# Decoder layer with 32 experts on one core: first norm applied in place, two more ring slots and one working slot lent to the weight ring's first turn, the loop for overfull experts moved from behind pair 3 to behind pair 11

## The chip, the cores and the metric

The kernel runs on one core of a Trainium2 chip. The metric is the device time of one execution in microseconds, as the median of three runs. All matrix work is in float32 or in a split float32 form, and all weights come from HBM once: 471 MB of them are read in one execution.

## The reference, cut to what matters

One attention sublayer and one mixture-of-experts sublayer, each followed by a layer norm. 256 tokens, 2048 features, 16 heads, 4 groups of 8 experts, 512 hidden features in an expert.

```
x = layer_norm(ALPHA * x + moba_attention(x, w_qkv, w_o), mix_ln_g, mix_ln_b)
# hierarchical_moe: best group of 4, then the best two of its 8 experts
comb = onehot_g[:, :, None] * e_gate[:, None, :]
for g in range(4):
    h = silu(einsum('td,edf->tef', xt, w_gate[g])) * einsum('td,edf->tef', xt, w_up[g])
    y = y + einsum('tef,efd->td', h * comb[:, g, :, None], w_down[g])
x = layer_norm(ALPHA * x + y, ffn_ln_g, ffn_ln_b)
```

So every token goes through 2 of 32 experts, 512 choices in all, and which tokens an expert gets is known only on the chip.

## The kernel before, in words

SBUF is cut into 24 slots of 128 x 2048 float32 (8 KB in each partition, 1 MB in all), named by tags (`slot`, L62). The attention half uses them for x, for its two split halves, for the heads' outputs, and seven of them as a ring for attention weights. The change is in the second half.

**The experts in pairs.** Sixteen pairs of experts run one after another (the loop `for p in range(NP)`). Each expert takes at most 64 tokens in this pass (CAP), so a pair fills 128 rows. One pair does, in TensorE's order: side 0's gate and up products in four steps j (`gate_up`, L511 to 516, tile gu), side 1's in four steps, the gather of the next pair's tokens in eight steps c2 (`gather`, L476, tiles pg and xg), the transpose of the hidden rows (hp, ht), and the down product in four steps k (L684, tile y). The rows of y are put back to their tokens by two more products for each half of the tokens (`add_rows`, `scatter`, tile cb) and added to the running sum; that is `rest(n)`, and it runs between the j steps of the next pair's side 0.

**The gather.** It is a matrix product: the normalised x is the stationary operand (the weights, 128 tokens by 128 features), and the 0/1 matrix o (tokens by slots, from `onehots`) is the moving one. Expert weights lie in HBM so that partition a of chunk (n, c) holds feature 512n + 4a + c. So the gather needs, as one weight block, the 128 features 4 apart. In the kernel before, ScalarE writes the normalised x to two other slots (xn, L404), and reads xs by steps of 4 so that each block lies in one run.

**The weight ring.** Each pair needs 24 pieces of 1 MB: 16 of gate and up, 8 of down; the last pair's down weights are 6 pieces of 1 MB and 4 of half of one. SP issues all their transfers in this order on one queue. `ring2` is 18 slots used in turn; `used(2)` behind each step of gate/up and each k of down gives two slots back, and `advance` issues the next pieces into them. An issue waits for the last reader of its slot, and for the transfer eight before it, since eight DMA semaphores are used in turn.

**The order.** TensorE and SP run in the written order from L647 on (`manual_schedule`); before it, the first pair's eight gathers and the count of overfull experts are written ahead of the pair loop and placed by the scheduler.

**The loop for overfull experts.** An expert with more than 64 tokens needs further passes (`further_passes`, L587). Their number is read on every engine; it is 0 for this input. The loop stands behind pair 3 (LOOP_AFTER = 2). Before it, all four rests of pair 3 run at once, four ring slots are kept free (LOOP_SLOTS), and all engines meet in a barrier.

**The rest.** `residual(j)` (L559) forms ALPHA * norm(x) + bias in xs, with rows of the norm's gain and bias made by TensorE (`rows_of`, L548); it runs in pair 1's side 0. The rows of the second norm (tiles r, copied to wv) are made in the last pair's side 1. "Pair 1" to "pair 16" count from one here; p in the code counts from zero.

Of the kernel before, what the change touches and what calls it, by code (L numbers as in the profile page):

```python
# [9 lines left out]
F32R = mybir.dt.float32r  # L10
# [17 lines left out]
WARM1 = (108, 16)  # L28
LOOP_AFTER = 2
LOOP_SLOTS = 4  # L30
# [8 lines left out]

S_XN, S_XG, S_YS = S_OH, 12, 13  # L40
S_EARLY, S_LATE = S_XH + S_XL + S_QK + (S_V,), S_OL + (14, S_TMP)
# [12 lines left out]
def hybrid_kernel(ctx: ExitStack, tc: tile.TileContext, x, w_qkv, w_o, ln1_g, ln1_b, w_grp, b_grp,  # L54
# [307 lines left out]
    done = (48 + sum(NCH * w // D for _, w in blocks)) % len(S_RING)  # L362
    ring2 = Rot(S_EARLY + S_RING[done:] + S_RING[:done] + S_LATE)
    n_ring = len(ring2.items)
# [8 lines left out]
    pieces += [(("v", 2, 0), None), (("v", 3, 0), None)]  # L373
# [3 lines left out]
    held, n_used = {}, 0  # L377

    def load(srcs, name, i=None):
        shape = [P, D] if srcs is None else list(srcs[0].shape) if len(srcs) == 1 else [P, len(srcs), *srcs[0].shape[1:]]  # L380
        t = slot(ring2() if i is None else i, shape, name)
# [4 lines left out]
    def advance(room=None):  # L386

        while len(held) < len(pieces) and len(held) - n_used < (room or n_ring):
            key, srcs = pieces[len(held)]
            held[key] = load(srcs, "w{}{}_{}".format(*key))  # L390

    def used(n, room=None):
        nonlocal n_used
        n_used += n
        advance(room)

# [159 lines left out]

    arstd = t2("arstd")

    def residual(n):  # L559

        cs = slice(n * 512, (n + 1) * 512)
        g_ = rows_of(0, n, yb[(2 * n) % 4], f"g1_{n}")
        b_ = rows_of(1, n, yb[(2 * n + 1) % 4], f"b1_{n}")
        for tt in range(NT):
            i = slice(tt, tt + 1)
            nc.vector.scalar_tensor_tensor(xs[tt][:, cs], xs[tt][:, cs], negmu[:, i], g_, op0=ALU.add, op1=ALU.mult)
            nc.vector.scalar_tensor_tensor(xs[tt][:, cs], xs[tt][:, cs], arstd[:, i], b_, op0=ALU.mult, op1=ALU.add)

    def gates():
# [13 lines left out]
        nc.vector.tensor_mul(gate, bc(ohg, GRP, EPG), le0.unsqueeze(2).to_broadcast([P, NT, GRP, EPG]))  # L583
        nc.vector.tensor_scalar_mul(arstd, rstd, ALPHA)
        return gate.rearrange("p t g e -> p t (g e)")

    def further_passes(free):  # L587

        ring = Rot(free[1:])
        n_pass = nc.values_load(passes_i[0:1, 0:1], min_val=0, max_val=8,  # L590
                                skip_runtime_bounds_check_because="512 choices in passes of 64 leave at most 7")
        with tc.For_i(0, n_pass, 1, iteration_sync="staggered"):  # L592
# [20 lines left out]
            one = bass.ds(er, 1)  # L613
            spare = slot(free[0], [P, 1024], "spare")
            xgx = spare.rearrange("p (n e s) -> p n e s", n=NCH, e=1)
# [21 lines left out]

    ys_all = slot(S_YS, [P, 2, 2, 512], "ys_all", F32R)
# [4 lines left out]
    gatef = gates()  # L643
    for tt in range(NT):
        nc.tensor.matmul(rps[:, 2, :], ones_b, selv[:, tt, :], start=tt == 0, stop=tt == 1)
    count_passes()
    order.enter_context(tc.manual_schedule(engines={mybir.EngineType.PE, mybir.EngineType.SP}))  # L647

    rest = None
    for p in range(NP):  # L650
        gu = [bank(gub(), [P, 512], f"gu{p}_{i}") for i in range(2)]
        hs = sm.tile([P, 512], F32, name=f"hs{p}", tag="ptv")
        for side in range(2):
            e = 2 * p + side
            for j in range(4):
                gate_up(gu[side], side, lambda c: xg[:, c, side], j, held["g", e, j], held["u", e, j])
                used(2, n_ring - (LOOP_SLOTS if p == LOOP_AFTER else 0))
# [18 lines left out]
        else:  # L676
            ht = transpose_hidden(hs, p)
        if p == NP - 1:
            break
        y = [bank(yb[n], [P, 512], f"y{p}_{n}") for n in range(4)]  # L680
        for k in range(4):
            for n in range(4):
                for side in range(2):
                    nc.tensor.matmul(y[n][sides[side]], ht[:, k, sides[side]], held["d", 2 * p + side, k][:, n * 512:(n + 1) * 512],  # L684
                                     start=k == 0, stop=k == 3, skip_group_check=True)
            used(2, n_ring - (LOOP_SLOTS if p == LOOP_AFTER else 0))

# [7 lines left out]
        if p == LOOP_AFTER:  # L695
            for n in range(4):
                rest(n)
            rest = None
            further_passes([ring2() for _ in range(LOOP_SLOTS)])
            ring2.n -= LOOP_SLOTS  # L700
            advance()
# [8 lines left out]
    def last_down(n):  # L710
# [7 lines left out]
        ys = slot((*S_XN, S_XG, S_YS)[n % 4], [P, 2, 512], f"ys{p}_{n}", F32R)  # L718
        split_rows(y, ys, width)
        lys.append(ys)  # L720

    def last_add(n):
        col, width = blocks[n]
        cs, ys = slice(col, col + width), lys[n]
        for tt in range(NT):
            cb = bank(last_cob(), [P, 512], f"cb{p}_{col}_{tt}")
            scatter(cb, ot, ys, tt, width)
            if n < ACT_STATS:
                st = stats2[:, tt, n]
                nc.vector.scalar_tensor_tensor(xs[tt][:, cs], cb[:, 0:width], 1.0, xs[tt][:, cs], op0=ALU.mult, op1=ALU.add,  # L730
                                               accum_out=sums[:, tt, n:n + 1])
                nc.vector.tensor_scalar_mul(st[:, 1:2], sums[:, tt, n:n + 1], 1.0 / width)
                nc.scalar.activation(cb[:, 0:width], xs[tt][:, cs], AF.Square, scale=-1.0, bias=st[:, 1:2], accum_out=st[:, 2:3])  # L733
            else:
                i = 2 * n - ACT_STATS
                nc.vector.tensor_add(xs[tt][:, cs], xs[tt][:, cs], cb[:, 0:width])
                nc.vector.bn_stats(stats2[:, tt, i:i + 2].rearrange("p a s -> p (a s)"), xs[tt][:, cs])

# [88 lines left out]
```

## Time and profile before

| | |
|---|---|
| median of 3 runs | 1403.14 us (1402.96 to 1406.17) |
| the profiled execution | 1405.03 us |
| its span, first to last instruction | 1403.3 us |
| TensorE busy in matmuls | 1348.7 us (96%) |
| VectorE, ScalarE, GpSimd busy | 450.5, 333.8, 16.3 us |
| granted TensorE clock, mean | 0.987 |
| DMA engines | 339 GB/s over the span, 421 GB/s in the second half |

The profile was taken in one execution, so its spans are compared with its own 1405.03 us; what lies outside the span is 1.7 us. A matmul's end is modelled, so 96% busy does not mean that TensorE has no slack: the chain of waits tells where it stood for a transfer. A float32 product is two passes, so the counts of rows in the trace are twice those of the code. DMA at 421 GB/s is the most that is seen over a long stretch.

### The profile page before, as it was taken

The page shows a single profiled execution, that of the slowest core. Times are in us where ns is not written, and L with a number is a line of the kernel's source. Part 1 is how long each engine was busy: PE and PEld are TensorE (multiplying, and loading weights), DVE is VectorE, ACT ScalarE, POOL GpSimd, SP SyncE. Part 2 cuts the span into 40 slices and gives each one's busy share as a digit, 9 for nine tenths or more (in the row PEclk, how much of TensorE's full clock was granted, in tenths as well). Part 3 has the DMA queues.
Part 4 walks back from the last instruction along what each step waited for, and adds up shares of the span by engine and source line. Part 5 has one row for each costly group of instructions (what it writes and reads, how often), then busy time and mean ns, then how long its engine had stood idle before and what let it go on. Part 6 is the DMA issues. An engine that isn't in the chain of part 4 may idle for free.

```text
span 1403.3 us, 17929 instructions
## 1 busy us (share of the span) xinstructions
PE 1348.7 (96%) x7537; PEld 807.7 (58%) x7537; DVE 450.5 (32%) x798; ACT 333.8 (24%) x567; POOL 16.3 (1%) x39
## 2 busy tenths in 40 slices
PE   9999999999999999979999999999999999998994
PEld 8999898988896534424344343443435434344442
DVE  5454645455454222221212212222122221212206
ACT  4454435345333101101011110110101101011123
POOL 0000100000000000000000000000000000000002
PEclk9999999999999999999999999999999999999997
DMA  9745455576555999989999999999999999999992
GB/s 340 239 151 182 148 171 190 180 262 239 176 200 218 365 421 421 421 357 421 421 421 421 420 421 421 421 421 421 421 421 421 421 421 421 421 421 421 420 382 71
DMA packets 103016, 475.52 MB, mean 339 GB/s; under 512 B 12756, under 2 KB 18964, under 8 KB 54804
## 3 DMA queue, kind: packets, MB, share of 16 engines
q1 hardware_dynamic: 102932, 474.33, 85.1%
q8 instruction: 61, 1.00, 0.3%
q14 instruction: 23, 0.19, 0.0%
HBM read 472.20 MB, written 2.10 MB: 338 GB/s over the span
## 4 chain that ended last, share of the span: by engine, by line
PE 41%; DMA 12%; DVE 2%; ACT 0%; issue 0%; DVEq 0%; SPq 0%; ACTq 0%
PE gu L516 19%; PE y L684 11%; DMA wu<-in_moe_w_up_dram 10%; PE pg L483 6%; PE cb L538 2%; DMA wd<-in_moe_w_down_dram 2%; PE cb L539 1%; PE y L716 1%; DVE xg L490 1%; PE r L553 1%; DVE xs L770 0%; DVE xs L760 0%; ACT cb L733 0%; DVE xs L756 0%; PE m L503 0%
## 5 line engine op out<-in xcount | busy, mean ns | idle before, releaser
L516 PE MATMUL gu<-wu,xg 128*64 128x512 f32 x1024 | 463.0, 599 | 16.1 <-DMA wu<-in_moe_w_up_dram 16.1
L516 PE MATMUL gu<-wg,xg 128*64 128x512 f32 x1024 | 462.1, 599 | 6.0 <-PEq L592 6.0
L516 PEld LDWEIGHTS gu<-wg,xg 128*64 128x64 f32 x1024 | 133.9, 137 | 205.6 <-issue 199.0
L684 PE MATMUL y<-wd,ht 128*64 128x512 f32 x960 | 209.3, 594 | 0.0
L516 PEld LDWEIGHTS gu<-wu,xg 128*64 128x64 f32 x1024 | 133.6, 137 | 90.1 <-issue 52.9
L160 PE MATMUL pj<-xh,ws 128*128 128x256 f32 x512 | 147.7, 288 | 0.8 <-ACT ws L150 0.8
L162 PE MATMUL pj<-xh,ws 128*128 128x256 f32 x512 | 147.3, 288 | 0.2 <-DVE ws L151 0.2
L161 PE MATMUL pj<-xl,ws 128*128 128x256 f32 x512 | 147.4, 288 | 0.0
L151 DVE TENSOR_TENSOR ws<-w,ws 128x1024 fp32r<-128x1024 f32 x88 | 107.8, 1225 | 122.2 <-ACT ws L150 122.2
L684 PEld LDWEIGHTS y<-wd,ht 128*64 128x64 f32 x960 | 67.6, 137 | 130.3 <-issue 127.9
L546 DVE TENSOR_TENSOR xs<-xs,cb 128x512 f32<-128x512 f32 x120 | 77.1, 683 | 192.6 <-PE cb L539 192.6
L483 PE MATMUL pg<-o,xn 128*128 128x128 f32 x1024 | 131.5, 281 | 4.3 <-DVE xg L490 2.4
L483 PEld LDWEIGHTS pg<-o,xn 128*128 128x128 f32 x1024 | 119.2, 191 | 28.4 <-issue 14.6
L150 ACT CAST ws<-w 128x1024 fp32r<-128x1024 f32 x88 | 92.4, 1050 | 135.1 <-PE pj L162 132.4
L532 ACT CAST ys_all<-y 128x512 fp32r<-128x512 f32 x60 | 35.1, 585 | 312.7 <-PE y L684 175.2
L521 DVE SCALAR_TENSOR_TENSOR hs<-hs,gs,gu 64x512 f32<-64x512 f32 x32 | 23.9, 747 | 239.2 <-ACT hs L520 237.9
L160 PEld LDWEIGHTS pj<-xh,ws 128*128 128x128 f32 x512 | 99.5, 194 | 1.2 <-ACT ws L150 1.0
L162 PEld LDWEIGHTS pj<-xh,ws 128*128 128x128 f32 x512 | 99.5, 194 | 0.8 <-DVE ws L151 0.6
L161 PEld LDWEIGHTS pj<-xl,ws 128*128 128x128 f32 x512 | 99.5, 194 | 0.1
L533 DVE TENSOR_TENSOR ys_all<-y,ys_all 128x512 fp32r<-128x512 f32 x60 | 41.2, 687 | 170.6 <-ACT ys_all L532 168.5
L490 DVE TENSOR_SCALAR xg<-pg,gbp 128x128 f32<-128x128 f32 x128 | 46.6, 405 | 91.9 <-PE pg L483 91.9
L520 ACT ACTIVATE hs<-gu 64x512 f32<-64x512 f32 x32 | 18.9, 591 | 218.1 <-PE gu L516 217.7
(196 smaller groups left out, 1251.9 us busy)
## 6 DMA issues: line engine op xcount, KB each, us to landing
wg<-in_moe_w_gate_dram SPq DMA_DIRECT2D x128, 1024.0 KB, 19.8
wu<-in_moe_w_up_dram SPq DMA_DIRECT2D x128, 1024.0 KB, 19.8
wd<-in_moe_w_down_dram SPq DMA_DIRECT2D x120, 1024.0 KB, 19.8
w<-in_attn_w_qkv_dram SPq DMA_DIRECT2D x44, 1024.0 KB, 5.1
wow<-in_attn_w_o_dram SPq DMA_DIRECT2D x16, 1024.0 KB, 5.2
wl<-in_moe_w_down_dram SPq DMA_DIRECT2D x6, 1024.0 KB, 17.2
wfirst<-in_attn_w_qkv_dram SPq DMA_DIRECT2D x3, 1024.0 KB, 11.3
xs<-in_x_dram SPq DMA_DIRECT2D x8, 256.0 KB, 8.6
```

What stands on the lines that cost most here:

```text
L150: nc.scalar.copy(t[:, 0, c], src[:, c])
L151: nc.vector.tensor_sub(t[:, 1, c], src[:, c], t[:, 0, c].bitcast(F32))
L160: nc.tensor.matmul(dst, ah, bh, start=start, stop=False, **kw)
L161: nc.tensor.matmul(dst, ah, bl, start=False, stop=False, **kw)
L162: nc.tensor.matmul(dst, al, bh, start=False, stop=stop, **kw)
L483: nc.tensor.matmul(pg[:, cc], xn[tt][:, n, c, :], o2[:, tt].rearrange("p e s -> p (e s)"), start=tt == 0, stop=tt == 1)
L490: nc.vector.tensor_scalar(to, pg[:, cc], g_, b_, op0=ALU.mult, op1=ALU.add)
L516: nc.tensor.matmul(gu[to], xg(4 * j + c), w[:, c, :], start=st, stop=sp, skip_group_check=True)
L532: nc.scalar.copy(ys[0:rows, 0, 0:width], y[0:rows, 0:width])
L533: nc.vector.tensor_sub(ys[0:rows, 1, 0:width], y[0:rows, 0:width], ys[0:rows, 0, 0:width].bitcast(F32))
L546: nc.vector.tensor_add(t, t, cb)
L684: nc.tensor.matmul(y[n][sides[side]], ht[:, k, sides[side]], held["d", 2 * p + side, k][:, n * 512:(n + 1) * 512], start=k == 0, stop=k == ...
```

## The change

- The first norm is written back into xs itself (in place). The gather's weight blocks are then 128 elements 4 apart (16 bytes) in xs.
- xn's two slots (6 and 7) and the slot of ys_all (13) join the ring for its first turn: 21 slots. They hold pieces 19 to 21 (down weights of pair 1), and are not given back: behind pair 1 they become acc (the running sum) and ys_all.
- `residual` forms ALPHA * g * xs + b in acc, in pair 2's side 0.
- The written order of TensorE and SP begins at the first gather. Four gather steps go ahead of the first gate/up step, two behind it, and two behind the second; the gates and the count of passes follow.
- The loop stands behind pair 11 (LOOP_AFTER = 10).
- The second norm's rows are made in pair 15, one behind each of its eight gate/up steps.
- VectorE empties the even gather steps and ScalarE the odd ones; before it was the other way round.
- The last pair's ys tiles take x's slots.

```
-LOOP_AFTER = 2
+LOOP_AFTER = 10
-S_XN, S_XG, S_YS = S_OH, 12, 13
+S_XG, S_SUM, S_YS = 12, S_OH, 13
...
-    ring2 = Rot(S_EARLY + S_RING[done:] + S_RING[:done] + S_LATE)
+    free = deque(S_EARLY + S_RING[done:] + S_RING[:done] + S_LATE + S_SUM + (S_YS,))
...
+        if pr == NP - 3:
+            pieces += [(("v", 2, 0), None), (("v", 3, 0), None)]
...
-        while len(held) < len(pieces) and len(held) - n_used < (room or n_ring):
+        while len(held) < len(pieces) and len(free) > keep:
             key, srcs = pieces[len(held)]
...
+    def used(*keys, keep=0):
+        free.extend(place[k] for k in keys if place[k] not in S_SUM + (S_YS,))
+        advance(keep)
...
-    xn = [slot(s, [P, 4, 4, P], f"xn{tt}") for tt, s in enumerate(S_XN)]
     for n in range(4):
         for tt in range(NT):
-            nc.scalar.activation(xn[tt][:, n], xs[tt][:, n * 512:(n + 1) * 512].rearrange("p (a c) -> p c a", c=4),
-                                 AF.Identity, scale=rstd[:, tt:tt + 1], bias=nmr[:, tt:tt + 1])
+            t = xs[tt][:, n * 512:(n + 1) * 512]
+            nc.scalar.activation(t, t, AF.Identity, scale=rstd[:, tt:tt + 1], bias=nmr[:, tt:tt + 1])
+    xn = [t.rearrange("p (n a c) -> p n c a", n=4, c=4) for t in xs]
...
-            if c2 % 2:
+            if c2 % 2 == 0:
                 nc.vector.tensor_scalar(to, pg[:, cc], g_, b_, op0=ALU.mult, op1=ALU.add)
...
-            nc.vector.scalar_tensor_tensor(xs[tt][:, cs], xs[tt][:, cs], negmu[:, i], g_, op0=ALU.add, op1=ALU.mult)
-            nc.vector.scalar_tensor_tensor(xs[tt][:, cs], xs[tt][:, cs], arstd[:, i], b_, op0=ALU.mult, op1=ALU.add)
+            nc.vector.scalar_tensor_tensor(acc[tt][:, cs], xs[tt][:, cs], ALPHA, g_, op0=ALU.mult, op1=ALU.mult)
+            nc.vector.tensor_add(acc[tt][:, cs], acc[tt][:, cs], b_)
...
-    for c2 in range(8):
+    for c2 in range(4):
         gather(c2, xg, o2, 0)
...
+                if p == side == 0 and j < 2:
+                    for c2 in (2 * j + 4, 2 * j + 5):
+                        gather(c2, xg, o2, 0)
+                if p == side == 0 and j == 1:
+                    gatef = gates()
+                    count_passes()
-                if p == 0 and side == 0:
+                if p == 1 and side == 0:
                     residual(j)
...
-                if p == NP - 1 and side == 1:
-                    for vec in (2, 3):
-                        nc.scalar.copy(held["v", vec, 0][:, j * 512:(j + 1) * 512], rows_of(vec, j, yb[vec], f"r2_{j}_{vec}"))
+                if p == NP - 2:
+                    vec = 2 + j % 2
+                    n = 2 * side + j // 2
+                    nc.scalar.copy(held["v", vec, 0][:, n * 512:(n + 1) * 512], rows_of(vec, n, mb(), f"r2_{n}_{vec}"))
```

Three places of the order show what moved. The first is TensorE at the start of pair 1: pg_N are the gather's steps, gu_0 the first expert's gate/up product from pieces wg_0 and wu_0, rps the count of choices, g_0 a row of the residual. The kernel before:

```order
L483 MATMUL pg_2_3978<-o_0_3960,xn_3897 128x128
L645 LDWEIGHTS ones_b
L645 MATMUL rps<-sel,ones_b 128x32
...
L516 MATMUL gu_0_4049<-wg_0_3860,xg_3963 64x512
L483 MATMUL pg_3_3985<-o_0_3960,xn_3896 128x128
...
L483 MATMUL pg_7_4013<-o_0_3960,xn_3897 128x128
L516 MATMUL gu_0_4049<-wg_0_3860,xg_3963 64x512
...
L553 MATMUL g_0_4064<-gb_896,ident 128x128 x4
L553 MATMUL b_0_4069<-gb_896,ident 128x128 x4
L516 MATMUL gu_0_4049<-wg_1_3864,xg_3963 64x512
```

The changed kernel, at the same place:

```order
L484 MATMUL pg_3_3989<-o_0_3964,xs_68 128x128
L640 LDWEIGHTS ones_b
L640 MATMUL rps<-sel,ones_b 128x32
...
L517 MATMUL gu_0_3998<-wg_0_3860,xg_3967 64x512
...
L484 MATMUL pg_4_4013<-o_0_3964,xs_67 128x128
...
L484 MATMUL pg_5_4020<-o_0_3964,xs_68 128x128
L517 MATMUL gu_0_3998<-wg_1_3864,xg_3967 64x512
```

The whole of step j = 0 now comes behind four gather steps, where before all eight lay ahead of its end; the residual's rows g and b are gone from here, and the weights of the gather are xs.

The second is SP at the loop, whose first row is the load of the number of passes; the rows above it are the last pieces issued ahead of it. The kernel before and then the changed one:

```order
L383 DMA wg_2_4869<-in_moe_w_gate_dram 128x2048
L383 DMA wu_2_4871<-in_moe_w_up_dram 128x2048
L590 TENSOR_LOAD passes_i
L592 COMPARE_AND_BRANCH
L592 UNCONDITIONAL_BRANCH
```

```order
L384 DMA wg_2_7043<-in_moe_w_gate_dram 128x2048
L384 DMA wu_2_7045<-in_moe_w_up_dram 128x2048
L587 TENSOR_LOAD passes_i
L589 COMPARE_AND_BRANCH
L589 UNCONDITIONAL_BRANCH
```

The same 14 pieces are issued ahead of the loop beyond those that were consumed (72 before, 264 now); the loop's place among the pieces moved by eight pairs.

The third is TensorE in the two last pairs, where r_0_2 and r_0_3 are the first rows of the second norm. The kernel before (pair 16, side 1) and then the changed one (pair 15, side 0):

```order
L516 MATMUL gu_1_8392<-wu_0_8269,xg_8273 64x512
L553 MATMUL r_0_2_8500<-gb_896,ident 128x128 x4
L553 MATMUL r_0_3_8506<-gb_896,ident 128x128 x4
L516 MATMUL gu_1_8392<-wg_1_8349,xg_8273 64x512
L516 MATMUL gu_1_8392<-wu_1_8351,xg_8273 64x512
```

```order
L539 MATMUL cb_0_1_8136<-ys_all,ot_7940 128x512
L540 MATMUL cb_0_1_8136<-ys_all,ot_7940 128x512
L554 MATMUL r_0_2_8142<-gb_896,ident 128x128 x4
L517 MATMUL gu_0_8117<-wg_1_7967,xg_7997 64x512
L517 MATMUL gu_0_8117<-wu_1_7969,xg_7997 64x512
```

The same 32 row products stand one pair earlier, one set of four behind a step instead of two.

## Rows read from the trace of the kernel before

**Rows 1.** Chain of waits, in order of time: start us, length us, what (xcount)

```profile
620.58 16.55 PE gu L516 x64
637.84 13.88 PE gu L516 x64
651.72 1.98 PE pg L483 x16
...
660.70 13.88 PE y L684 x64
674.58 3.43 PE gu L516 x16
...
693.88 13.88 PE gu L516 x64
...
932.85 1.98 PE pg L483 x16
...
1149.53 19.81 DMA wu<-in_moe_w_up_dram
...
1293.82 1.98 PE pg L483 x16
```

**Rows 2.** Stretches: us, then PE, PEld, DVE, ACT, POOL busy, granted clock, DMA share, GB/s

```profile
420.00:430.00 10.00, 8.30 (x115) 7.82 (x113) 3.94 (x17) 8.75 (x10) 0.00 (x0) 1.00 0.55 230
430.00:440.00 10.00, 10.00 (x60) 6.00 (x58) 3.27 (x15) 3.71 (x9) 0.00 (x0) 1.00 0.00 0
...
480.00:490.00 10.00, 10.00 (x54) 4.50 (x56) 0.73 (x2) 1.12 (x3) 0.00 (x0) 1.00 0.75 297
...
610.00:620.00 10.00, 3.21 (x11) 1.33 (x10) 4.75 (x8) 0.59 (x1) 0.00 (x0) 0.95 0.69 287
620.00:630.00 10.00, 9.42 (x32) 3.27 (x34) 0.49 (x2) 0.00 (x0) 0.20 (x4) 0.71 0.83 329
...
700.00:800.00 100.00, 99.64 (x511) 44.48 (x508) 21.58 (x43) 14.44 (x30) 0.00 (x0) 1.00 1.01 421
```

**Rows 3.** DMA issues of the page: xcount, KB each, median us to landing

```profile
wg<-in_moe_w_gate_dram SPq DMA_DIRECT2D x128, 1024.0 KB, 19.8
```

**Rows 4.** TensorE in order of time, pair 1: start us, length us, what, xcount

```profile
424.80 2.00 PE L483 MATMUL pg<-o,xn 128*128 128x128 f32 x16
...
439.04 0.59 PE L516 MATMUL gu<-wu,xg 128*64 128x512 f32 x1
...
481.84 13.95 PE L684 MATMUL y<-wd,ht 128*64 128x512 f32 x64
```

**Rows 5.** The loop behind pair 3, in order of time: SP, TensorE, VectorE

```profile
601.39 0.38 SPq L383 DMA_DIRECT2D wu<-in_moe_w_up_dram  x1
...
607.74 0.50 PE L538 MATMUL cb<-ys_all,ot 128*128 128x512 f32 x1
...
614.65 0.69 DVE L546 TENSOR_TENSOR xs<-xs,cb 128x512 f32<-128x512 f32 x1 [0.30 <-PE cb L539]
...
620.60 0.34 SPq L383 DMA_DIRECT2D wg<-in_moe_w_gate_dram  x1
```

**Rows 6.** TensorE in pair 16, one of four sets of rows

```profile
1339.47 2.05 PE L553 MATMUL r<-gb,ident 16*128 16x128 f32 x16
```

**Rows 7.** Groups by line and shape, 0 to 460 us: busy us, mean ns, idle before

```profile
L404 ACT ACTIVATE xn<-xs,nmr,rstd 128x512 f32<-128x512 f32 x8 | 9.7, 1302 | 0.0
...
L483 PEld LDWEIGHTS pg<-o,xn 128*128 128x128 f32 x64 | 7.5, 191 | 4.3 <-issue 2.4 <-ACT xg L492 1.9
...
L516 PEld LDWEIGHTS gu<-wg,xg 128*64 128x64 f32 x36 | 4.4, 136 | 6.9 <-issue 6.3
...
L553 PEld LDWEIGHTS b<-gb,ident 16*128 16x128 f32 x32 | 3.9, 185 | 0.0
...
L150 ACT CAST ws<-wfirst 128x512 fp32r<-128x512 f32 x4 | 2.4, 619 | 0.1
```

More of the change, by code (lines that the diff above doesn't have):

```diff
@@ L1 @@
+from collections import deque
 from contextlib import ExitStack, nullcontext
@@ L372, in hybrid_kernel @@
                 pieces += [(("d", e, k), [wd_v[e, k]]) for e in (2 * pr, 2 * pr + 1)]
-    pieces += [(("v", 2, 0), None), (("v", 3, 0), None)]
     for n, (col, width) in enumerate(blocks):
@@ L376, in hybrid_kernel, with load @@
         pieces += [(("l", n, i), [src]) for i, src in enumerate(srcs)] if width == 512 else [(("l", n, 0), srcs)]
-    held, n_used = {}, 0
-    def load(srcs, name, i=None):
+    held, place = {}, {}
+    def load(srcs, name, i):
         shape = [P, D] if srcs is None else list(srcs[0].shape) if len(srcs) == 1 else [P, len(srcs), *srcs[0].shape[1:]]
-        t = slot(ring2() if i is None else i, shape, name)
+        t = slot(i, shape, name)
         for k, src in enumerate(srcs or []):
@@ L384, in load, with advance @@
         return t
-    def advance(room=None):
-        while len(held) < len(pieces) and len(held) - n_used < (room or n_ring):
+    def advance(keep=0):
+        while len(held) < len(pieces) and len(free) > keep:
             key, srcs = pieces[len(held)]
[L390 to L395, printed above, removed]
+            place[key] = free.popleft()
+            held[key] = load(srcs, "w{}{}_{}".format(*key), place[key])
+    def used(*keys, keep=0):
+        free.extend(place[k] for k in keys if place[k] not in S_SUM + (S_YS,))
+        advance(keep)
     advance()
-    xn = [slot(s, [P, 4, 4, P], f"xn{tt}") for tt, s in enumerate(S_XN)]
     for n in range(4):
         for tt in range(NT):
-            nc.scalar.activation(xn[tt][:, n], xs[tt][:, n * 512:(n + 1) * 512].rearrange("p (a c) -> p c a", c=4),
-                                 AF.Identity, scale=rstd[:, tt:tt + 1], bias=nmr[:, tt:tt + 1])
+            t = xs[tt][:, n * 512:(n + 1) * 512]
+            nc.scalar.activation(t, t, AF.Identity, scale=rstd[:, tt:tt + 1], bias=nmr[:, tt:tt + 1])
+    xn = [t.rearrange("p (n a c) -> p n c a", n=4, c=4) for t in xs]
     def bc(a, *shape):
@@ L544, in add_rows @@
             scatter(cb, ot, ys, tt, rows=rows)
-            t = xs[tt][:, n * 512:(n + 1) * 512]
+            t = acc[tt][:, n * 512:(n + 1) * 512]
             nc.vector.tensor_add(t, t, cb)
@@ L555, in rows_of @@
         return t
-    arstd = t2("arstd")
     def residual(n):
         cs = slice(n * 512, (n + 1) * 512)
-        g_ = rows_of(0, n, yb[(2 * n) % 4], f"g1_{n}")
-        b_ = rows_of(1, n, yb[(2 * n + 1) % 4], f"b1_{n}")
+        g_ = rows_of(0, n, mb(), f"g1_{n}")
+        b_ = rows_of(1, n, mb(), f"b1_{n}")
         for tt in range(NT):
-            i = slice(tt, tt + 1)
-            nc.vector.scalar_tensor_tensor(xs[tt][:, cs], xs[tt][:, cs], negmu[:, i], g_, op0=ALU.add, op1=ALU.mult)
-            nc.vector.scalar_tensor_tensor(xs[tt][:, cs], xs[tt][:, cs], arstd[:, i], b_, op0=ALU.mult, op1=ALU.add)
+            nc.vector.scalar_tensor_tensor(acc[tt][:, cs], xs[tt][:, cs], ALPHA, g_, op0=ALU.mult, op1=ALU.mult)
+            nc.vector.tensor_add(acc[tt][:, cs], acc[tt][:, cs], b_)
     def gates():
@@ L583, in gates, with further_passes @@
         nc.vector.tensor_mul(gate, bc(ohg, GRP, EPG), le0.unsqueeze(2).to_broadcast([P, NT, GRP, EPG]))
-        nc.vector.tensor_scalar_mul(arstd, rstd, ALPHA)
         return gate.rearrange("p t g e -> p t (g e)")
-    def further_passes(free):
-        ring = Rot(free[1:])
+    def further_passes(slots):
+        ring = Rot(slots[1:])
         n_pass = nc.values_load(passes_i[0:1, 0:1], min_val=0, max_val=8,
@@ L613, in further_passes @@
             one = bass.ds(er, 1)
-            spare = slot(free[0], [P, 1024], "spare")
+            spare = slot(slots[0], [P, 1024], "spare")
             xgx = spare.rearrange("p (n e s) -> p n e s", n=NCH, e=1)
@@ L636, in further_passes @@
                 add_rows("x", n, ot, ysx, (yb[n],) * NT, CAP)
-    ys_all = slot(S_YS, [P, 2, 2, 512], "ys_all", F32R)
+    order.enter_context(tc.manual_schedule(engines={mybir.EngineType.PE, mybir.EngineType.SP}))
     o2 = onehots(0)
     xg = slot(S_XG, [P, NCH, 2, CAP], "xg0")
-    for c2 in range(8):
+    for c2 in range(4):
         gather(c2, xg, o2, 0)
[L643 to L649, printed above, removed]
+    nc.tensor.matmul(rps[:, 2, :], ones_b, selv[:, 0, :], start=True, stop=False)
+    nc.tensor.matmul(rps[:, 2, :], ones_b, selv[:, 1, :], start=False, stop=True)
+    gatef, ys_all, acc, rest = None, None, None, None
     for p in range(NP):
+        keep = LOOP_SLOTS if p == LOOP_AFTER else 0
         gu = [bank(gub(), [P, 512], f"gu{p}_{i}") for i in range(2)]
@@ L656, in hybrid_kernel @@
                 gate_up(gu[side], side, lambda c: xg[:, c, side], j, held["g", e, j], held["u", e, j])
-                used(2, n_ring - (LOOP_SLOTS if p == LOOP_AFTER else 0))
-                if p == 0 and side == 0:
+                used(("g", e, j), ("u", e, j), keep=keep)
+                if p == side == 0 and j < 2:
[5 more added lines that the diff above has]
+                if p == 1 and side == 0:
                     residual(j)
@@ L685, in hybrid_kernel @@
                                      start=k == 0, stop=k == 3, skip_group_check=True)
-            used(2, n_ring - (LOOP_SLOTS if p == LOOP_AFTER else 0))
+            used(("d", 2 * p, k), ("d", 2 * p + 1, k), keep=keep)
+        if p == 0:
+            ys_all = slot(S_YS, [P, 2, 2, 512], "ys_all", F32R)
+            acc = [slot(s, [P, D], f"acc{tt}") for tt, s in enumerate(S_SUM)]
         def rest(n, p=p, y=y, ot=ot):
@@ L698, in hybrid_kernel @@
             rest = None
-            further_passes([ring2() for _ in range(LOOP_SLOTS)])
-            ring2.n -= LOOP_SLOTS
+            further_passes(list(free)[:LOOP_SLOTS])
             advance()
@@ L717, in last_down @@
                                  stop=k == 3, skip_group_check=True)
-        ys = slot((*S_XN, S_XG, S_YS)[n % 4], [P, 2, 512], f"ys{p}_{n}", F32R)
+        ys = slot((*S_X, S_XG, S_YS)[n % 4], [P, 2, 512], f"ys{p}_{n}", F32R)
         split_rows(y, ys, width)
@@ L729, in last_add @@
                 st = stats2[:, tt, n]
-                nc.vector.scalar_tensor_tensor(xs[tt][:, cs], cb[:, 0:width], 1.0, xs[tt][:, cs], op0=ALU.mult, op1=ALU.add,
+                nc.vector.scalar_tensor_tensor(acc[tt][:, cs], cb[:, 0:width], 1.0, acc[tt][:, cs], op0=ALU.mult, op1=ALU.add,
                                                accum_out=sums[:, tt, n:n + 1])
                 nc.vector.tensor_scalar_mul(st[:, 1:2], sums[:, tt, n:n + 1], 1.0 / width)
-                nc.scalar.activation(cb[:, 0:width], xs[tt][:, cs], AF.Square, scale=-1.0, bias=st[:, 1:2], accum_out=st[:, 2:3])
+                nc.scalar.activation(cb[:, 0:width], acc[tt][:, cs], AF.Square, scale=-1.0, bias=st[:, 1:2], accum_out=st[:, 2:3])
             else:
                 i = 2 * n - ACT_STATS
-                nc.vector.tensor_add(xs[tt][:, cs], xs[tt][:, cs], cb[:, 0:width])
-                nc.vector.bn_stats(stats2[:, tt, i:i + 2].rearrange("p a s -> p (a s)"), xs[tt][:, cs])
+                nc.vector.tensor_add(acc[tt][:, cs], acc[tt][:, cs], cb[:, 0:width])
+                nc.vector.bn_stats(stats2[:, tt, i:i + 2].rearrange("p a s -> p (a s)"), acc[tt][:, cs])
     for n in range(len(blocks)):
@@ L751, in part @@
         cs = slice(n * 512, (n + 1) * 512)
-        return xs[tt][:, cs], g2[:, cs], b2[:, cs]
+        return acc[tt][:, cs], g2[:, cs], b2[:, cs]
     def centre(tt, n):
@@ L773, in store @@
     def store(tt, n):
-        nc.sync.dma_start(out=out_v[tt][:, n * 512:(n + 1) * 512], in_=xs[tt][:, n * 512:(n + 1) * 512])
+        nc.sync.dma_start(out=out_v[tt][:, n * 512:(n + 1) * 512], in_=acc[tt][:, n * 512:(n + 1) * 512])
     for tt in range(NT):
```

2 lines of the change are left out of this document (removed).

## The prediction

> **What bounds the kernel now.** I read the chain of waits first, then the stretches, then the order in time around the holes that these showed. The chain [rows 1] has two parts. In the fourth to the eighth pair it is all TensorE: a pair is side 0 with the four rests 19.30 us (674.58 to 693.88), side 1 13.88, gather and transpose 8.98 (651.72 to 660.70), down 13.88; together 56.04. From the ninth to the fourteenth pair transfers of wu stand in the chain (one row of six such pairs is shown), and the gathers of pairs 9 and 15 are 360.97 us apart (932.85 to 1293.82), which is 60.16 for a pair. That is the DMA's pace: at 421 GB/s (the stretch from 700 to 800 [rows 2]) a piece of 1.0486 MB takes 2.49 us, 24 of them 59.7. So TensorE is 4.1 us a pair faster than the weights, it starts with a lead of stored weights to work off, and what counts is when the stream of weights is through: any time in which the DMA stands still is lost for good, and any work of TensorE before the end is free up to 4.1 us a pair.
>
> The stream stands still in three places [rows 2]. With 230 GB/s in 420 to 430 and none in 430 to 440 it has one long hole, from about 425.5 to 441: all 18 slots are full and nothing is consumed. With 297 GB/s it loses 10 x (1 - 297/421) = 2.9 us in 480 to 490, the last time that the ring is full while TensorE gathers. At the loop it loses 3.2 + 2.2 = 5.4 us (610 to 630). Everything behind the last wait, from 1293.82 to 1403.3, is TensorE's chain and the final norm.
>
> **The change part by part.** *The start and the ring's first turn.* Four gather steps are half of eight; one costs about 1.0 us (8 passes of 1.98/16 us [rows 1]). So step j = 0 ends at 424.80 [rows 4] + 4.1 + 0.2 for the count + 3.43 [rows 1] = 432.5; before it ended at 439.6 (439.04 + 0.59). The first slots are given back 7.1 us earlier, and three more pieces, 7.5 us of transfer, fill the time before. The hole of some 15.5 us shrinks to about 1. But that is not the gain: the three slots are not given back, so the ring holds 18 again, and the residual's rows now slow pair 2. What counts is the last moment at which the ring is full. Before it was the first k of pair 1's down: 481.84 [rows 4] + 3.47 = 485.3, and with 24 pieces of 2.49 the stream would reach the same place one pair later at 545.0. In the changed kernel I step TensorE through: 432.5, + 2.05 (two gather steps) + 3.43 + 2.05 + 6.86 = 446.9; the slots' products 1.0; side 1 13.88; gather 8.98; down 13.88: pair 2 begins at 484.6. Its side 0 is 19.30 + four sets of rows at 2.05 [rows 6] = 27.5, then 13.88 + 8.98 + 3.47: 538.4. The ring is full there for the last time. The gain is 545.0 - 538.4 = 6.6 us.
>
> *Costs at nothing.* The residual's 16 VectorE instructions, the norm in place, the swapped emptying of pg and the last ys in x's slots: VectorE is busy 22 of 100 us and ScalarE 14 (700 to 800 [rows 2]), so they lie beside TensorE; in pair 2 VectorE has about 5 us of work in steps of 6.7. Without that cover a step would be some 2 us longer, 8 us in all, and the gain of this term would be gone. The norm reads its source in one run, so I expect about 0.62 us for an instruction instead of 1.30 (ScalarE's cast of the same shape [rows 7]); its 5.4 us lie ahead of the gather's second half and are in the times above.
>
> *The loop.* Its barrier waits for TensorE, VectorE and SP. Before, SP had issued its last piece at 601.39 and went on at 620.60 [rows 5]; the last sum ended at 615.3, so the barrier and the branch took 5.2. Eight transfers in flight last 19.8 us [rows 3] if all eight are there; there were fewer, hence the hole. Behind pair 11 TensorE waits for weights anyway. SP's last issue ahead of the loop waits for the transfer eight before it, which is the sixth behind the last piece of pair 11: 6 x 2.49 = 14.9 us later, while TensorE and VectorE need 3.5 for the last k and some 8 to 9 for the four rests (607.74 to 615.3). SP comes last, waits for almost nothing and goes on 5.2 us later with seven or eight transfers still under way. The 5.4 us are saved. If the queue did run dry, the price is these 5.4 again. TensorE loses there 620.58 - 607.74 = 12.8, + 16.55 - 13.7 = 2.8 since the granted clock fell (0.71 in 620 to 630 [rows 2]), less the rests that side 0 then lacks (5.4): 10.2 us. At 4.1 a pair that is made up in pairs 12 to 14.
>
> *The second norm's rows.* Eight sets of 1.03 us [rows 6] = 8.2 leave pair 16, which nothing covers, and go to pair 15, of which 4.1 are covered by the wait for weights. Gain 4.1.
>
> *Sum:* 6.6 + 5.4 + 4.1 = 16.1. The profiled execution's 1405.03 becomes 1388.9. The runs' median lies 1.9 below that execution, so I predict 1387.0.
>
> *The gather's weights by steps of 16 bytes: the unknown price.* It hits 64 passes in each of 16 pairs. One weight load of 128 columns takes 191 ns, one of 64 takes 136 [rows 7]: 0.86 ns a column, 110 for 128, and a pass of the gather takes 124, so the load lies just under its cover. No row shows TensorE reading weights by steps. The lower end is nothing, or a little below (ScalarE's shorter norm is already counted). The nearest row of TensorE is the weight load for the norm's rows, which reads one column 128 times: 185 ns, as for a run [rows 7]. That is no step of 16 bytes, but it is the same engine and operation off the plain run. The nearest row with the step itself is ScalarE's norm, 1302 ns against 619 for a cast of the same shape: twice. I take the first, as the row of the same engine, without much trust, and keep the second as the other end.
>
> Against it stands a rule of the Trainium skill: SBUF — State Buffer, section Specifications (TRN2), says that SBUF serves lines of 16 bytes and that full bandwidth needs at least two hits on a line. Steps of four float32 hit each line once. ScalarE's 1302 ns agree with it. By that rule the load's columns would take longer here, which is the first rival below.
>
> **The rivals.** *Slower: the strided loads cost double.* 110 ns become 220, the pass at least 220, which is 96 more; 64 of them are 6.1 us a pair, above the 4.1 that are covered. Then TensorE never waits again and its own chain is the time: 1403.3 - 24.7 (six pairs of 60.16 against 56.04) - 2.9 (pair 2's down begins at 535.0 instead of 537.9) = 1375.7; the loop and the second norm's rows only move. With 16 x 6.1 = 97.6 this is a span of 1473, and about 1473 for a median. By ScalarE's own ratio (2.1) the load is 231 and the time 1485. It decides from 27.6/16 = 1.7 us a pair, 27 ns a pass. For it: ScalarE's row, and a load that has no cover to spare. Against it: no row of TensorE.
>
> *No difference: the gains are paid back.* The queue runs dry at the loop (5.4 back) and VectorE holds pair 2 up (6.6 back); what is left is 4.1, 1399. For it: SP stood 19 us at the loop before, as long as a full queue lasts. Against it: behind pair 11 nobody but SP is late, and VectorE has 5 us to do in 6.7. One of the two alone gives 1392 to 1394, still faster.
>
> *Faster than forecast: TensorE is still working off its lead at pair 11.* Then the stream does not matter and the time is TensorE's 1375.7 of span, 1376 or so. For it: the ring's lead is larger without the loop at pair 3.
>
> **How the numbers follow.** Forecast 0.52, 1387, its own range 1379 to 1396 (one of the paid-back terms above, half of the last rival below). Faster still 0.04. Paid back, 0.06, split over 1396 to 1403. Strided loads dear, 0.38, of which some 0.25 lie below 1485 and the rest above. To leave out no more than 0.2 the range must take in the doubled load: 1378 to 1485. A measurement of this kernel tells 0.3% from no change, that is 1398.9 to 1407.3. Faster by more: 0.52 + 0.04 + 0.02 = 0.58. Within: 0.04 of the paid-back case and 0.01 of small prices of the load, 0.05. Slower: 0.37.
>
> **What would show it.** In the changed profile the gather's 48 passes ahead of the transpose should take some 6.2 us, with weight loads of 191 ns; at 11 us and 300 ns the first rival has it, the chain is all TensorE, and no transfer of wu stands in it. The stretch 430 to 440 should show DMA near 421 GB/s, the loop (near 1060 to 1080) no loss, pairs in the middle 59.7 to 60.2 apart, pair 16's side 1 13.9 without rows. I am wrong if the pairs are 62 or more apart, or if the stream is steady and the end is not earlier by what the holes gave.

## The result, and the profile after

The changed kernel takes 1490.24 us (median of 4 runs, 1485.7 to 1491.64) against 1404.66 for the kernel before (median of 4 beside it): 1.0603 times, 95% interval 1.0574 to 1.0633. The forecast of 1387.0 is wrong. What came is its first rival, whose own time was 1473 to 1485; the end lies just above the range's 1485.

The page of the changed kernel gives the groups of the gate products and of the gather over the whole execution. Columns: what, count, busy us, mean ns of one, idle before it.

```profile
L517 PE MATMUL gu<-wg,xg 128*64 128x512 f32 x1024 | 455.6, 595 | 2.8 <-PEq L589 2.8
...
L484 PEld LDWEIGHTS pg<-o,xs 128*128 128x128 f32 x1024 | 241.5, 328 | 23.6 <-issue 13.0
L484 PE MATMUL pg<-o,xs 128*128 128x128 f32 x1024 | 247.8, 401 | 6.9 <-ACT xg L493 6.9
...
wg<-in_moe_w_gate_dram SPq DMA_DIRECT2D x128, 1024.0 KB, 11.3
```

A weight load of the gather takes 328 ns where [rows 7] had 191. The gate products waited for nothing but the loop's branch (2.8 us in all). A piece of weights now lands 11.3 us after its issue; in [rows 3] it took 19.8, about what eight pieces take one after another (8 x 2.49 = 19.9). The chain of waits (start us, length us, what), which answers to [rows 1], from pair 11's loop to pair 14 and the start of pair 16's side 1:

```profile
1150.83 13.95 PE gu L517 x64
...
1165.49 13.88 PE gu L517 x64
1179.37 11.41 PE pg L484 x48
...
1190.81 0.82 ACT xg L493 x2
...
1191.67 4.00 PE pg L484 x16
1195.67 13.88 PE y L684 x64
1209.55 3.43 PE gu L517 x16
...
1242.74 11.41 PE pg L484 x48
...
1306.10 11.41 PE pg L484 x48
...
1428.17 13.91 PE gu L517 x64
```

No transfer stands in it. From one gather to the next it is 63.36 us (1242.74 to 1306.10), and all but 0.9 of it is TensorE at work; in those 0.9 its last gather step waits for ScalarE to empty an earlier one (1190.78 to 1191.67; before, it was VectorE, for 0.8). The gather with the transpose takes 16.30 (1179.37 to 1195.67) instead of 8.98, the products are as long as before (13.88). 7.32 more in each of 16 pairs is 117 us, of which about 20 fill time in which TensorE waited for weights before (experiment 1, with plain runs, is 98 us faster). The stretches, with the columns of [rows 2]:

```profile
420.00:430.00 10.00, 10.00 (x93) 9.93 (x91) 3.46 (x13) 3.29 (x6) 0.00 (x0) 1.00 1.01 421
430.00:440.00 10.00, 10.00 (x47) 6.45 (x49) 0.78 (x3) 1.62 (x4) 0.00 (x0) 1.00 0.57 215
...
480.00:490.00 10.00, 9.87 (x44) 5.87 (x46) 0.73 (x2) 1.36 (x4) 0.00 (x0) 1.00 0.28 88
700.00:800.00 100.00, 99.54 (x446) 50.29 (x447) 22.68 (x46) 11.15 (x23) 0.00 (x0) 1.00 0.98 406
...
1140.00:1150.00 10.00, 6.24 (x22) 2.60 (x18) 7.00 (x12) 1.34 (x3) 0.00 (x0) 1.00 0.26 108
```

The lent slots do fill the first hole (421 GB/s in 420 to 430, and half of the next stretch). Then the stream waits for slots: even from 700 to 800, where it had 421, it has 406. The last row is the loop. The kernel has changed its bound, from the weights' stream to TensorE. ScalarE's norm, now read in one run, is shorter, at 805 ns instead of the 1302 of [rows 7]:

```profile
L405 ACT ACTIVATE xs<-xs,nmr,rstd 128x512 f32<-128x512 f32 x8 | 5.8, 805 | 0.0
```

### The profile page after: what moved, and what is told of

Its sections match the earlier page's. It is cut to its first block, busy times and chain, and to the rows that moved or that the text cites. A ratio compares the mean times of both kernels' runs of the same rounds, so it can differ in the third digit from the quotient of the medians.

```text
span 1483.9 us, 17935 instructions
## 1 busy us (share of the span) xinstructions
PE 1446.6 (97%) x7537; PEld 918.7 (62%) x7537; DVE 449.7 (30%) x797; ACT 328.9 (22%) x567; POOL 16.3 (1%) x39
## 5 line engine op out<-in xcount | busy, mean ns | idle before, releaser
L517 PE MATMUL gu<-wg,xg 128*64 128x512 f32 x1024 | 455.6, 595 | 2.8 <-PEq L589 2.8
L517 PE MATMUL gu<-wu,xg 128*64 128x512 f32 x1024 | 455.6, 595 | 0.0
L484 PEld LDWEIGHTS pg<-o,xs 128*128 128x128 f32 x1024 | 241.5, 328 | 23.6 <-issue 13.0
L484 PE MATMUL pg<-o,xs 128*128 128x128 f32 x1024 | 247.8, 401 | 6.9 <-ACT xg L493 6.9
L547 DVE TENSOR_TENSOR acc<-acc,cb 128x512 f32<-128x512 f32 x120 | 77.1, 684 | 181.8 <-PE cb L540 181.8
L493 ACT ACTIVATE xg<-pg,gbp 128x128 f32<-128x128 f32 x128 | 51.7, 454 | 212.5 <-PE pg L484 212.5
## 6 DMA issues: line engine op xcount, KB each, us to landing
wg<-in_moe_w_gate_dram SPq DMA_DIRECT2D x128, 1024.0 KB, 11.3
```

The lines of the kernel that those rows point to most:

```text
L517: nc.tensor.matmul(gu[to], xg(4 * j + c), w[:, c, :], start=st, stop=sp, skip_group_check=True)
```

## The experiments

My theory after the result: the step of 16 bytes is the whole loss, and the rest of the change is worth what the forecast's three terms say. The rival: the order, the lent slots or the loop's place costs something.

**1. The changed kernel with plain runs.**

```
-    xn = [t.rearrange("p (n a c) -> p n c a", n=4, c=4) for t in xs]
+    xn = [t.rearrange("p (n c a) -> p n c a", n=4, c=4) for t in xs]
```

> The changed kernel, with each weight block of the gather read as 128 neighbouring elements of xs instead of 128 elements 4 apart; the expert weights are left as they are, so the gathered features stand in another order than the weights' rows and only the time is read. Theory (the step of 16 bytes is the whole loss): a gather's weight load falls from 328 to about 191 ns, a pass from 238 to about 124 to 128, gather and transpose from 16.3 to about 9 us, the transfers of wu come back into the chain, pairs 59.7 to 60.2 apart, time 1385 to 1391 (the sum of the three terms of the forecast, 16.1 us). Rival (something else of the change costs it: the order of the start, the lent slots, the place of the loop): 1475 to 1490.

1392.64 us, 0.9911 (0.9893 to 0.9929) of the kernel before. The group of the gather's weight loads, by form:

```profile
L484 PEld LDWEIGHTS pg<-o,xs 128*128 128x128 f32 x1024 | 120.3, 191 | 31.7 <-issue 13.2 <-ACT xg L493 9.3 <-DVE xg L491 7.3
```

191 ns, and 98 us of the changed kernel's time are gone with one line. The step is what the loss hangs on. The time is 1.6 us above what was expected; the sum of the terms was somewhat too large (below).

**2. The kernel before with steps.** ScalarE writes xn in one run to its own slots, and the gather reads it 4 apart.

```
-    xn = [slot(s, [P, 4, 4, P], f"xn{tt}") for tt, s in enumerate(S_XN)]
+    xn = [slot(s, [P, D], f"xn{tt}") for tt, s in enumerate(S_XN)]
...
-            nc.scalar.activation(xn[tt][:, n], xs[tt][:, n * 512:(n + 1) * 512].rearrange("p (a c) -> p c a", c=4),
+            nc.scalar.activation(xn[tt][:, n * 512:(n + 1) * 512], xs[tt][:, n * 512:(n + 1) * 512],
...
+    xn = [t.rearrange("p (n a c) -> p n c a", n=4, c=4) for t in xn]
```

> The kernel before, in which ScalarE writes the normalised x to its two slots in one run and the gather reads its weight blocks from there by steps of 4 elements; nothing else is changed. Theory: weight load 328 ns instead of 191, gather and transpose 16.3 instead of 9.0 us, TensorE's own chain 1375.7 + 2.9 of span plus 16 x 7.3 = 117, so about 1495 of time, with ScalarE's norm at about 0.8 us instead of 1.3. Rival (the step is not what costs): 1400 to 1405.

1494.1 us, 1.0632 (1.0613 to 1.0651), as expected; its weight loads take 329 ns. So the step alone does it, without anything else of the change.

**3. The norm in its own slots, all else changed.** 19 slots in the first turn instead of 21, the running sum in xs.

```
-    free = deque(S_EARLY + S_RING[done:] + S_RING[:done] + S_LATE + S_SUM + (S_YS,))
+    free = deque(S_EARLY + S_RING[done:] + S_RING[:done] + S_LATE + (S_YS,))
...
+    xn = [slot(s, [P, 4, 4, P], f"xn{tt}") for tt, s in enumerate(S_XN)]
...
-            nc.scalar.activation(t, t, AF.Identity, scale=rstd[:, tt:tt + 1], bias=nmr[:, tt:tt + 1])
-    xn = [t.rearrange("p (n a c) -> p n c a", n=4, c=4) for t in xs]
+            nc.scalar.activation(xn[tt][:, n], xs[tt][:, n * 512:(n + 1) * 512].rearrange("p (a c) -> p c a", c=4),
+                                 AF.Identity, scale=rstd[:, tt:tt + 1], bias=nmr[:, tt:tt + 1])
...
-            acc = [slot(s, [P, D], f"acc{tt}") for tt, s in enumerate(S_SUM)]
+            acc = xs
```

> The changed kernel, with the normalised x written by ScalarE to its own two slots, each weight block in one run, as before; only the slot of ys_all is then lent to the ring's first turn (19 slots), and the running sum stays in xs. Order, loop behind pair 11 and the second norm's rows are as changed. Theory: the two lent slots gain little, since the last moment at which the ring is full lies in pair 2; 1386 to 1391, faster than both kernels. Rival (the 21 slots carry the start's gain of 6.6 us): 1393 to 1396. Rival (something else of the change costs it): 1475 or more.

1390.7 us, 0.9902 (0.9886 to 0.9919): 1% faster than the kernel before, and faster than the changed one. The two lent slots gain nothing that shows: without them the time is not longer than in experiment 1. A gain of 2 us or so could be hidden, since the two versions also differ in the norm's and the running sum's slots and in the pace of their streams (below).

**4. Steps of 8 bytes.** Each weight block is 128 elements 2 apart.

```
-    xn = [t.rearrange("p (n a c) -> p n c a", n=4, c=4) for t in xs]
+    xn = [t.rearrange("p (n a c) -> p n c a", c=2, a=P) for t in xs]
...
-            n, c = divmod(2 * c2 + cc, 4)
+            n, c = divmod(2 * c2 + cc, 2)
```

> The changed kernel, with each weight block of the gather as 128 elements 2 apart (8 bytes); the gathered features then stand in another order than the weights' rows, and only the time is read. If the price is that of lines of 16 bytes of which only one element is used, a step of 2 uses each line twice: weight load about 191 ns, time 1385 to 1391. If every step that is not a plain run has one price: 328 ns, 1490. If the price grows with the distance: in between, some 240 to 260 ns, 1400 to 1440.

1392.69 us, 0.9912 (0.9892 to 0.9931): the time of the plain runs of experiment 1, and like it a little above what was expected (1.7 us).

**7. Steps of 64 bytes**, the same edit with 16 in place of 2, one run:

> The changed kernel, with each weight block of the gather as 128 elements 16 apart (64 bytes) instead of 4 apart; the gathered features then stand in another order than the weights' rows, and only the time is read. If the price is one more access for an element that lies on a line of its own: the same load as at 4 apart, 328 ns, and 1490 us. If the price grows with the distance: more than 328 ns, a time above 1500.

1470.57 us, which is neither of the two expected: the price does not grow with the distance, it is a little less than at 16 bytes. The weight loads of experiments 4 and 7:

```profile
L484 PEld LDWEIGHTS pg<-o,xs 128*128 128x128 f32 x1024 | 126.6, 196 | 30.2 <-issue 13.0 <-ACT xg L493 10.0 <-DVE xg L491 5.8
```

```profile
L484 PEld LDWEIGHTS pg<-o,xs 128*128 128x128 f32 x1024 | 226.0, 311 | 23.6 <-issue 13.0 <-ACT xg L493 10.5
```

So 191, 196, 328 and 311 ns at steps of 4, 8, 16 and 64 bytes. The price is not for every step, nor does it grow with the distance: it comes in somewhere above 8 and at or below 16 bytes. Why 64 is cheaper than 16 stays open.

**5. Experiment 3 with the loop back behind pair 3.**

```
-LOOP_AFTER = 10
+LOOP_AFTER = 2
```

> The version with the normalised x in its own slots (1390.7 us), with the loop put back behind pair 3. Theory (the forecast's loop term): the hole of 5.4 us in the stream of weights is back, 1395 to 1397, and the stretches at 610 to 640 show some 290 to 330 GB/s. Rival (the stream makes it up, or the loop costs the same behind pair 11): 1390 to 1392.

1400.08 us, 0.9971 (0.9959 to 0.9984): 9.7 us more than experiment 3 by the two ratios, not 5.4. The stretches at the loop, and SP's transfers around it (start us, length us):

```profile
600.00:610.00 10.00, 9.66 (x44) 3.26 (x40) 2.15 (x4) 1.71 (x3) 0.00 (x0) 1.00 1.01 420
610.00:620.00 10.00, 3.88 (x12) 1.78 (x12) 5.48 (x9) 0.63 (x2) 0.00 (x0) 0.96 0.35 143
620.00:630.00 10.00, 8.64 (x30) 3.02 (x32) 0.49 (x2) 0.00 (x0) 0.20 (x4) 0.70 0.76 297
```

```profile
602.11 0.38 SPq L384 DMA_DIRECT2D wu<-in_moe_w_up_dram  x1
621.37 0.34 SPq L384 DMA_DIRECT2D wg<-in_moe_w_gate_dram  x1
```

The hole is 6.6 + 2.9 = 9.5 us. SP goes on at 621.37, and in the kernel before at 620.60 [rows 5]: nearly the same moment, though the stream came to the loop 3.5 us further on (the table below). When the barrier opens does not follow the stream here; with the same number of pieces issued ahead, a stream that is ahead runs dry earlier and waits longer. So a loop behind pair 3 takes back nearly all that the new start gained. It can't be told to the last microsecond: in this execution the granted clock was also 0.83 in 510 to 520, with TensorE busy throughout the stretch before, so part of those 10 us ran at the lower level (1.2 GHz) and some 1.7 us of work were lost; in experiment 3 it was 1.00.

**6. Experiment 3 with the second norm's rows back in pair 16.**

```
-                if p == NP - 2:
-                    vec = 2 + j % 2
-                    n = 2 * side + j // 2
-                    nc.scalar.copy(held["v", vec, 0][:, n * 512:(n + 1) * 512], rows_of(vec, n, mb(), f"r2_{n}_{vec}"))
+                if p == NP - 1 and side == 1:
+                    for vec in (2, 3):
+                        nc.scalar.copy(held["v", vec, 0][:, j * 512:(j + 1) * 512], rows_of(vec, j, yb[vec], f"r2_{j}_{vec}"))
```

> The version with the normalised x in its own slots, with the second norm's rows made in the last pair's side 1 as before. Theory (the forecast's third term): pair 16 is 7.9 us longer (four sets of 1.98) and pair 15 gets back only what the wait for weights did not cover, about 4; together 1394 to 1396. Rival (pair 15 has no wait to cover them, since TensorE is just behind the stream there): no change, 1390 to 1392.

1393.51 us, 0.9926 (0.9909 to 0.9943). By the ratios 3.4 us more than experiment 3, somewhat under the 4 expected, and the two intervals overlap. The profiled spans are 4.8 apart (1391.3 and 1386.5), but not all of it is the rows: with the rows in pair 16 its side 1 takes 9.0 us more until ScalarE begins on hs, pair 15 takes 6.5 less, and the other 2.3 fall behind them, where the granted clock was 0.59 in 1350 to 1355 (1.00 in experiment 3) and 32 products of the last down took 8.89 us instead of 7.09. Experiment 1, without rows there, has these slow products too (8.78). So the rows' place is worth about 2.5 in these two profiles: the term is likely there, but smaller than forecast, and these rounds don't prove it.

**8. Experiment 3 with the residual taken out of pair 2.**

```
-            nc.vector.tensor_add(t, t, cb)
+            if name == 0:
+                nc.vector.tensor_copy(t, cb)
+            else:
+                nc.vector.tensor_add(t, t, cb)
...
-            i = slice(tt, tt + 1)
-            nc.vector.scalar_tensor_tensor(xs[tt][:, cs], xs[tt][:, cs], negmu[:, i], g_, op0=ALU.add, op1=ALU.mult)
-            nc.vector.scalar_tensor_tensor(xs[tt][:, cs], xs[tt][:, cs], arstd[:, i], b_, op0=ALU.mult, op1=ALU.add)
+            r = sm.tile([P, P, 4], F32, name=f"res{n}_{tt}", tag="ptv")
+            nc.vector.scalar_tensor_tensor(r, xn[tt][:, n].rearrange("p c a -> p a c"), ALPHA,
+                                           g_.rearrange("p (a c) -> p a c", c=4), op0=ALU.mult, op1=ALU.mult)
+            nc.vector.tensor_add(acc[tt][:, cs], acc[tt][:, cs], r.rearrange("p a c -> p (a c)"))
+            nc.vector.tensor_add(acc[tt][:, cs], acc[tt][:, cs], b_)
...
-                if p == 1 and side == 0:
+                if p == 8 and side == 0:
                     residual(j)
```

> The version with the normalised x in its own slots, with the residual taken out of pair 2: the first pair's rows are written to the running sum instead of added, and the residual is added in pair 9's side 0, read from the normalised x by steps (three VectorE instructions for a part instead of two). Theory (the stream is lost as long as the ring is full, and the last such moment is pair 2's down): pair 2's down begins 8.2 to 8.5 us earlier, the holes at 500 to 550 shrink by as much, and the time falls to 1381 to 1385, unless TensorE's own chain (some 1378) ends last. Rival (the holes ahead of pair 3 are not what sets the end): 1389 to 1392. Rival (the late residual holds TensorE up in pair 9 and the lead is used up): 1390 or more.

1383.9 us, 0.9852 (0.9835 to 0.9868), the fastest of all, as expected. Pair 2's down begins at 528.05 instead of 535.41. Two stretches of experiment 3, and the same two here:

```profile
510.00:520.00 10.00, 9.54 (x47) 3.89 (x48) 4.70 (x10) 0.96 (x2) 0.00 (x0) 1.00 0.76 300
...
530.00:540.00 10.00, 9.61 (x63) 6.12 (x63) 1.81 (x6) 2.89 (x7) 0.00 (x0) 1.00 0.75 310
```

```profile
510.00:520.00 10.00, 10.00 (x53) 3.98 (x50) 0.48 (x1) 0.59 (x1) 0.00 (x0) 1.00 1.01 422
...
530.00:540.00 10.00, 10.00 (x48) 3.30 (x46) 0.00 (x0) 0.49 (x1) 0.00 (x0) 1.00 1.01 420
```

The two holes in pair 2 (2.9 and 2.6 us) are gone, and nothing of them is paid back later: from 425 to 575 the stream gains 12.0 us on the kernel before, where experiment 3 gains 5.3 (the table below).

**9. The kernel before with the loop behind pair 11,** the edit of experiment 5 the other way round.

> The kernel before with the loop behind pair 11 and nothing else changed. Theory (what a loop behind pair 3 costs is the lead that the stream has there: TensorE, not the stream, sets when it goes on): the hole of 5.4 us at 610 to 630 is gone and no other takes its place, 1397.5 to 1399.5; then the new start is worth the rest of the 13 us only together with the later loop. Rival (the loop costs the stream as much behind pair 11, and its move is worth nothing): 1403 to 1405. Rival (the loop's place alone carries the gain of 9.4 us that the version with its own slots lost when the loop was put back): 1393 to 1395.

1399.52 us, 0.9970 (0.9959 to 0.9980), at the upper end of what was expected. The hole at the loop is gone and the new place makes none:

```profile
610.00:620.00 10.00, 10.00 (x44) 3.61 (x42) 3.77 (x6) 1.17 (x2) 0.00 (x0) 1.00 1.02 423
620.00:630.00 10.00, 10.00 (x48) 4.24 (x46) 3.78 (x9) 0.97 (x2) 0.00 (x0) 1.00 1.02 420
...
1080.00:1090.00 10.00, 6.46 (x24) 2.34 (x26) 0.49 (x2) 0.00 (x0) 0.20 (x4) 0.83 1.02 419
```

The loop's place alone is worth about 4 us; its 9.7 us in experiment 5 are about these and the new start's gain, which it had taken back.

## Why the prediction was wrong, step by step

**The step that failed** is "the gather's weights by steps of 16 bytes: the unknown price". I took the lower end, nothing, by the weight load for the norm's rows (185 ns [rows 7]), "as the row of the same engine". That row reads one column 128 times. It has a step of zero and never leaves its place, so it says nothing of a step of 16 bytes; the row that had the property in question was ScalarE's. Measured on both engines the price is nearly the same: TensorE (328 - 191) / 128 = 1.07 ns a column, ScalarE (1302 - 805) / 512 = 0.97 ns an element. What the working needed was this difference for one element, carried from one engine to the other. It would have given 124 ns on a load that had 14 ns of cover under a pass of 124, so some 110 ns a pass, 7.0 us a pair; measured are 7.32. The plain row that this needs was in the trace of before already, in ScalarE's part of the second norm (800 ns):

```profile
L765 ACT ACTIVATE xs<-xs,nmr,rstd 128x512 f32<-128x512 f32 x5 | 3.6, 800 | 0.6 <-DVE nmr L783 0.6
```

The rule that I weighed holds here: the Trainium skill, SBUF — State Buffer, section Specifications (TRN2), wants two hits on a line of 16 bytes. The traces agree: experiment 4 has two hits and pays 5 ns a load, the changed kernel has one and pays 137.

I gave the rival 0.38, though the nearest sound row, ScalarE's, spoke for it.

**The rival's size.** It said 6.1 us a pair and 1473, or 1485 by a ratio of 2.1 taken from ScalarE; 7.32 a pair came, and 1490. The ratio itself was worked out against a cast (619 ns); the norm in one run takes 805, so ScalarE's ratio is 1.6, and that of TensorE's load is 1.7. That its 1485 comes near the measured span of 1483.9 is in part luck: its 107 ns a pass are 7.5 us too little in all, and its chain is 8.9 too long. The chain that it started from, 1375.7, gives 1375.7 + 117 = 1492.8, and the span is 1483.9. It still held the loop at its old cost to TensorE (10.2 us). In the changed kernel TensorE stands 2.8 us at the branch; the granted clock is 1.00 in the stretch of the loop (1140 to 1150), and the side 0 behind it takes 13.95 instead of the 16.55 of [rows 1]. By the working's own sum the loop costs 9.7 (1141.17 to 1150.83) - 5.4 = 4.3 us there. Another 3.3 come at the end: from TensorE's last product in pair 16's side 1 to the end of the span it is 41.8 us, before 45.1.

**The other three terms** are seen in experiments 1 and 3, where the stream bounds the kernel again. The lead of the stream over the kernel before, in us at 420 GB/s, worked out by adding up what the stretches of 5 us moved up to a moment:

| lead at | 425 us | 575 us | 650 us | 1250 us |
|---|---|---|---|---|
| experiment 1 (21 slots) | 1.7 | 6.0 | 11.0 | 8.8 |
| experiment 3 (19 slots) | 1.2 | 6.5 | 11.7 | 11.6 |
| experiment 5 (loop behind pair 3) | 0.0 | 3.5 | -0.7 | -0.7 |
| experiment 8 (residual late) | -0.2 | 11.8 | 16.9 | 16.7 |

- *Start and first turn*, 6.6: measured 4.3 and 5.3 (from 425 to 575). The place was right: pair 2's down begins at 535.74 in experiment 1 and 535.48 in experiment 3 (535.0 in the working), and experiment 8 shows that the residual there is what keeps the ring full. In experiment 1 the near hit is in part luck. Its step j = 0 begins at 427.16 and ends some 1.9 us earlier than in the working, and then the granted clock is 0.83 in 510 to 520, a part at the lower level (1.2 GHz) right behind 10 us in which TensorE was busy for 9.76; that costs 1.7. Without it the 4.3 may have been up to 6.0.
- *Loop*, 5.4: measured 5.0 and 5.2 (575 to 650), and no loss behind pair 11. But the term isn't independent of the first: experiments 5 and 9 show that with the loop behind pair 3 the start's gain is worth next to nothing. The prediction added the two as if each stood alone; their sum holds only because both were made.
- *Second norm's rows*, 4.1: 3.4 by the ratios, not clear of noise, and about 2.5 in the two profiles of experiments 3 and 6. There pair 15 pays 6.5 us for the rows, so the wait for weights covers 1.7 of their 8.2, not 4.1. Pair 16's side 1 takes 13.91 without rows, as forecast.

Together experiment 3 gains 14.5 us by its median (1405.19 to 1390.7; 13.8 by the ratio) where the sum said 16.1, and experiment 1 gains 12.5. The forecast lay another 1.9 lower, since the three runs shown of before had a median below the profiled execution; with seven runs beside experiment 3 it was 1405.19, and that step was no more than the runs' scatter.

**What stays open.** In experiment 1 the stream is 0.4% slower to the end, and its lead falls from 11.0 to 8.8. Experiment 1 and then experiment 3, from 1100 to 1200:

```profile
1100.00:1200.00 100.00, 98.69 (x510) 44.32 (x506) 21.47 (x43) 14.22 (x30) 0.00 (x0) 1.00 1.01 419
```

```profile
1100.00:1200.00 100.00, 98.70 (x507) 44.56 (x504) 21.58 (x43) 14.23 (x30) 0.00 (x0) 1.00 1.01 421
```

Experiment 4, the other one with the norm in place, has the slower stream too (its lead falls from 10.2 to 7.9); experiments 3, 5, 6, 8 and 9 don't. Whether the place of xs and of the running sum does it, or each execution's own pace, was not tried.

## What to carry to other kernels

When no row shows the price of an access pattern on one engine, take the row that shows the pattern, on whichever engine, as a difference for each element, before one that shows the engine without the pattern. Then see what cover the operation has: here 14 ns, in a place that is run 1024 times. And where a stream is ahead of its reader, a barrier that the reader opens can take the lead back, as behind pair 3 here; a gain made ahead of such a barrier then counts only once the barrier is moved.

## What the runs showed that I had not expected

- A weight load with a step of 64 bytes is cheaper than one of 16 (311 against 328 ns, 1470.57 against 1490.24 us).
- VectorE paid for a far step as well: in experiment 8 its product of the residual, which reads xn 512 bytes apart, takes 1033 ns. In the changed kernel the same product with xs read in one run takes 684. Experiment 8, then the changed kernel:

```profile
L570 DVE SCALAR_TENSOR_TENSOR res<-xn,g 128x512 f32<-128x512 f32 x8 | 8.3, 1033 | 5.5 <-PE g L557 5.5
```

```profile
L564 DVE SCALAR_TENSOR_TENSOR acc<-xs,g 128x512 f32<-128x512 f32 x8 | 5.5, 684 | 11.5 <-PE g L554 11.5
```

- TensorE's half clock behind the loop is no constant of the loop: the granted clock was 0.70 in 620 to 630 of experiment 5, a part of it at the lower level (1.2 GHz), and 1.00 (2.4 GHz) in 1140 to 1160 of the changed kernel. TensorE had stood 6.1 us at the branch in the first and 2.8 in the second. Nor is such a fall bound to standing still: it was 0.66 in 1125 to 1130 of the changed kernel, with TensorE busy for 4.5 of the 5 us before and all of these. What decides it was not tried.
